# Expert stage: weight rows without a split are split like the rest, every sixth low part goes to GpSimd, and results are added in groups of three pairs

## The chip, the cores and the metric

The kernel runs on one core of one Trainium2 chip, as one program in one launch. The metric is the device time of that program in microseconds (us). Kernels are compared by the median of several runs.

## The reference

The model has two blocks. The change is in the last part of the first: sixteen experts, each of which takes the 64 tokens of 512 that the router rates highest for it.

```
logits = jnp.einsum('bnd,de->ben', xn, router_w).astype(jnp.float32)
aff = jax.nn.softmax(logits, axis=1)
gate, idx = lax.top_k(aff, cap)                                   # cap = 64
xg = jax.vmap(lambda xs, ix: xs[ix])(xn, idx)                     # 16 experts x 64 x 1024
hid = jax.nn.silu(jnp.einsum('becd,edf->becf', xg, w_gate)) * jnp.einsum('becd,edf->becf', xg, w_up)
y = jnp.einsum('becf,efd->becd', hid, w_down) * gate[..., None].astype(xn.dtype)
scatter = lambda ix, ys: jnp.zeros((n, d), ys.dtype).at[ix.reshape(-1)].add(ys.reshape(-1, d))
return jax.vmap(scatter)(idx, y)
```

All matrices are 1024 x 1024 in float32, three for each expert (`w_gate`, `w_up`, `w_down`). The result, scaled, is added to the residual `h` (512 x 1024). Behind it stand a norm and the second block, two layers of attention and feed-forward, which the change does not touch.

## The kernel before

A float32 product is made from rounded halves: a value x is split into a high part, x rounded to the format `F32R`, and a low part, x minus the high part. TensorE then multiplies the `F32R` parts.

**The experts' weights.** 48 matrices come in rows of 128 x 1024 (512 KB), here called chunks: 8 to a matrix, 24 to an expert, 384 in all. `stream` sets their order, and `moe_load` sends each on the SP queue into one of 19 raw buffers (tiles `mraw`, `raw`, `PT`, `rawx`, `moewk`). `moe_w` takes the next chunk and splits it: ScalarE (ACT) writes the high part (`whi`, `mwhi`), VectorE (DVE) or GpSimd (POOL) subtracts it from the raw chunk to get the low part (`wlo`, `mwlo`). There are four buffer pairs for these parts (three with tag `w`, one with tag `mw`), so that chunk n takes over the pair of chunk n - 4. After a split, the next load is issued into the freed raw buffer.

**Who makes the low part.** A counter n numbers the split chunks. The first five low parts and each with n % `MPOOL` == `MPOOL` - 1 are GpSimd's, the others VectorE's. With `MPOOL` = 9 these are 42 and 294 of 336.

**The direct chunks.** The third chunk of each matrix (k = 2, `DIRECT = (2,)`) isn't split. Its 48 products are made in plain float32 from the raw chunk (64 rows of output), with the unsplit tokens in `XD` or the unsplit hidden values in `hs`; the chunk's raw buffer is free when TensorE has read it.

**The products.** `moe_mm` makes, for each split chunk, four products 128 x 512: the stationary operand holds the high parts of the 64 tokens in its first 64 columns and their low parts in the rest (`XS` for gate and up, `HS` for down). `hidden` adds the two halves while it transposes (product with `J`), applies silu and multiplies; `down` adds the halves with one ACT copy and one VectorE addition for each half of a row (`zt`, `z`).

**Adding to the residual.** Two experts make a pair. `pair_rows` scales the pair's rows, splits them (`yh`, `yl`) and builds a 0/1 matrix (`oht`) that places rows at their tokens. `combine` sums over the pairs in the list `Y` in PSUM, for each of 4 token tiles and 2 halves, and VectorE adds the sum to `h`. `GROUPS = (1, 5, 9, 13)` names the experts behind which this is done: after one pair, then after two pairs, three times; the eighth pair is added in `b2_entry`, the first step of the second block (`add`, then norm, then the first projection).

The program is written in that order, and a scheduling step orders each engine's instructions by its own estimate; waits between engines follow from the data. The stage below is the stretch from 711 to 1275 us of the trace: from the first product of an expert to the last.

Of the kernel before, what the change touches and what calls it, by code (L numbers as in the profile page):

```python
# [8 lines left out]
F32 = mybir.dt.float32  # L9
F32R = mybir.dt.float32r  # L10
# [12 lines left out]
MRAW = 7  # L23
AFTER = (0, 1, 2, 3)
RAWS = MRAW + 12
DIRECT = (2,)
MPOOL = 9
GROUPS = (1, 5, 9, 13)
CAP = 64
EPS = 1e-6  # L30
LN_EPS = 1e-5
# [6 lines left out]
class Net:  # L38
# [904 lines left out]
    def moe_w(self, *key):  # L943

        nc = self.nc
        got, raw = self.raws.pop(0)
        assert got == key
        if key[2] in DIRECT:
            return raw, None
        n = self.cw  # L950
        self.cw += 1
        P, tag, bufs = (self.wp, "w", 3) if n % 4 < 3 else (self.mw, "mw", 1)
        hi = P.tile([128, 1024], F32R, name=tag + "hi", tag=tag + "hi", bufs=bufs)
        lo = P.tile([128, 1024], F32R, name=tag + "lo", tag=tag + "lo", bufs=bufs)
        nc.scalar.copy(hi, raw)  # L955
        eng = nc.gpsimd if n < 5 or n % MPOOL == MPOOL - 1 else nc.vector
        eng.tensor_tensor(lo, raw, hi.bitcast(F32), OP.subtract)  # L957
        self.moe_load()
        return hi, lo
# [27 lines left out]
    def xs_pair(self):  # L987

        nc, mo = self.nc, self.mo2
        XS = [mo.tile([128, 8, 128], F32R, name="XS%d" % i, tag="XS", bufs=3) for i in range(2)]  # L990
        XD = mo.tile([128, max(1, len(DIRECT)), 2, 64], F32, name="XD", tag="XD", bufs=2)
        for q in range(2):
            pt = self.aux()
            for k in range(4):
                o = (4 * q + k) * 128
                nc.tensor.transpose(pt[:, k * 128:(k + 1) * 128], self.xg[:, o:o + 128], self.ident)
            p4 = pt.rearrange("p (k e s) -> p k e s", k=4, e=2)
            ks = slice(4 * q, 4 * q + 4)
            for j, k in enumerate(DIRECT):
                if k // 4 == q:  # L1000
                    nc.scalar.copy(XD[:, j], p4[:, k % 4])
            for i in range(2):
                nc.scalar.copy(XS[i][:, ks, 0:64], p4[:, :, i])
                nc.vector.tensor_tensor(XS[i][:, ks, 64:128], p4[:, :, i], XS[i][:, ks, 0:64].bitcast(F32), OP.subtract)
        return [(XS[i], {k: XD[:, j, i] for j, k in enumerate(DIRECT)}) for i in range(2)]

    def moe_mm(self, wn, e, X, X32):
        nc = self.nc
        pp = [self.mm(), self.mm()]
        for k in range(8):  # L1010
            wh, wl = self.moe_w(wn, e, k)
            for q in range(2):
                c = slice(q * 512, (q + 1) * 512)
                if wl is None:
                    nc.tensor.matmul(pp[q][0:64], X32[k], wh[:, c], start=False, stop=False)
                    continue
                nc.tensor.matmul(pp[q], X[:, k], wh[:, c], start=k == 0, stop=False)  # L1017
                nc.tensor.matmul(pp[q], X[:, k], wl[:, c], start=False, stop=k == 7)  # L1018
            if wl is None:
                self.moe_load()  # L1020
        return pp

    def hidden(self, e, X):

        nc, mo = self.nc, self.mo2
        V = nc.vector
        fT = []
        for m, wn in enumerate(("w_gate", "w_up")):
            pp = self.moe_mm(wn, e, *X)
            g = self.wk[:, 1 + m]  # L1030
            nc.scalar.copy(g[:, 0:512], pp[0])
            nc.scalar.copy(g[:, 512:1024], pp[1])
            pf = self.aux()
            for k in range(8):
                nc.tensor.matmul(pf[:, k * 64:(k + 1) * 64], g[:, k * 128:(k + 1) * 128], self.J, start=True, stop=True)
            fT.append(pf)
        s = mo.tile([128, 512], F32, name="hs", tag="hs", bufs=2)
        nc.scalar.activation(s, fT[0], AF.Silu)
        V.tensor_tensor(s, s, fT[1], OP.mult)
        HS = mo.tile([128, 8, 128], F32R, name="HS", tag="HS", bufs=2)  # L1040
        s3 = s.rearrange("p (k n) -> p k n", k=8)
        nc.scalar.copy(HS[:, :, 0:64], s3)
        V.tensor_tensor(HS[:, :, 64:128], s3, HS[:, :, 0:64].bitcast(F32), OP.subtract)
        return HS, {k: s3[:, k] for k in DIRECT}

    def down(self, e, HS):

        nc, mo = self.nc, self.mo2
        pp = self.moe_mm("w_down", e, *HS)
        if e % 2 == 0:  # L1050
            self.z = mo.tile([128, 1024], F32, name="z", tag="z", bufs=1)
        r = slice(64 * (e % 2), 64 * (e % 2) + 64)
        for q in range(2):
            t = mo.tile([64, 512], F32, name="zt", tag="zt", bufs=1)
            nc.scalar.copy(t, pp[q][64:128])
            nc.vector.tensor_tensor(self.z[r, q * 512:(q + 1) * 512], pp[q][0:64], t, OP.add)

    def pair_rows(self, p):

        nc, mo = self.nc, self.mo2  # L1060
        V = nc.vector
        z = self.z
        yh = mo.tile([128, 1024], F32R, name="yh", tag="yh", bufs=2)
        yl = mo.tile([128, 1024], F32R, name="yl", tag="yl", bufs=2)
        V.scalar_tensor_tensor(z, z, self.gd[:, p:p + 1], self.g2, op0=OP.mult, op1=OP.mult)
        nc.scalar.copy(yh, z)
        V.tensor_tensor(yl, z, yh.bitcast(F32), OP.subtract)
        pb = self.aux()
        for s in range(2):
            sel = self.s16[0:16, 2 * p + s:2 * p + s + 1].to_broadcast([16, 64])  # L1070
            nc.tensor.matmul(pb[64 * s:64 * s + 64], sel, self.posT[0:16].bitcast(F32), start=True, stop=True)
        oht = mo.tile([128, 512], F32R, name="oht", tag="oht", bufs=2)
        V.tensor_scalar(oht, pb, self.rowi, None, op0=OP.is_equal)
        return yh, yl, oht

# [10 lines left out]
    def experts(self):  # L1086
# [17 lines left out]
        def finish(e):  # L1104
# [3 lines left out]
            Y.append(self.pair_rows(e // 2))  # L1108
            if e not in GROUPS:
                return  # L1110
# [734 lines left out]
    def ffn(self, l):  # L1845
# [18 lines left out]
        def ready(k):  # L1864
            kept[k] = hidden(k)
# [6 lines left out]
        for q in range(2):  # L1872
# [4 lines left out]
            def mms(t, i, w, kks=(0, 1)):  # L1877
                ts = slice(t * 128, (t + 1) * 128)
                for kk in kks:
                    k, o = 2 * i + kk, slice(kk * 512, (kk + 1) * 512)  # L1880
                    h = w[2 + kk]
                    self.mm3(ps[t], h[0][:, ts], h[1][:, ts], w[0][:, o], w[1][:, o], k == 0, k == 21)

            rows = lambda i: (hidden(2 * i), hidden(2 * i + 1))
            for i in range(last):
                h = rows(i)
# [189 lines left out]
```

## Time and profile before

| | |
|---|---|
| runs | 3185.0 us median of three (3178.12 to 3187.54) |
| profiled execution | 3183.61 us, of which span 3181.8 us |
| TensorE (PE) busy over the span | 3039.0 us (96%) |
| VectorE (DVE) | 2247.8 us (71%) |
| ScalarE (ACT) | 1587.9 us (50%) |
| GpSimd (POOL) | 379.9 us (12%) |
| granted TensorE clock, mean | 0.981 of full |

Busy time of an engine is the time in which at least one of its instructions ran. These shares are means over stages that differ: what the change is worth is read from the expert stage alone, some 18% of the span. A wait for several things is put down to the one that came last.

### The profile page before, as it was taken

How to read it: one execution, taken by the hardware profiler on the slowest of the kernel's cores; microseconds unless marked ns; L12 is line 12 of the kernel's file. 1: busy time of each engine (PE TensorE's matmuls, PEld its weight loads, DVE VectorE, ACT ScalarE, POOL GpSimd, SP SyncE). 2: the span in 40 equal slices, each digit the busy share in tenths (PEclk: the TensorE clock that was granted, in tenths of full speed). 3: DMA queues.
4: the chain of work that ended last, by engine and by line, in shares of the span. 5: the costliest groups of instructions: out<-in, count | busy, mean ns of one | idle time of the engine just before them, and what ended most of it. 6: DMA issues, size and time to landing. Idle time of an engine off the chain costs nothing. (4 is left out here: it accounts for less than half of the span.)

```text
span 3181.8 us, 43471 instructions
## 1 busy us (share of the span) xinstructions
PE 3039.0 (96%) x16242; PEld 2477.6 (78%) x16242; DVE 2247.8 (71%) x3782; ACT 1587.9 (50%) x2711; POOL 379.9 (12%) x295
## 2 busy tenths in 40 slices
PE   7999999969999999699999999999999999999998
PEld 4888777756655666678787789998878777789986
DVE  7778665468988888777565488873676655688854
ACT  6445432228766776365353435551465444445541
POOL 1454200032112121200011000000000011000000
PEclk9999999979999999899999999999999999999999
DMA  5112245549999997311215333332312224333332
GB/s 196 54 47 71 83 143 192 198 179 396 374 345 342 350 370 271 101 62 58 87 56 166 97 117 99 109 105 93 106 54 74 76 93 148 100 106 107 107 100 79
DMA packets 140781, 470.05 MB, mean 148 GB/s; under 512 B 16269, under 2 KB 20365, under 8 KB 140569
## 3 DMA queue, kind: packets, MB, share of 16 engines
q1 hardware_dynamic: 139416, 463.08, 41.7%
q0 software_dynamic: 1152, 4.19, 0.4%
q8 instruction: 127, 2.08, 0.3%
q14 instruction: 86, 0.70, 0.1%
HBM read 456.71 MB, written 10.50 MB: 147 GB/s over the span
## 5 line engine op out<-in xcount | busy, mean ns | idle before, releaser
L107 DVE TENSOR_TENSOR wlo<-raw,whi 128x1024 fp32r<-128x1024 f32 (+4 forms) x340 | 379.9, 1120 | 306.4 <-ACT whi L106 305.0
L106 ACT CAST whi<-raw 128x1024 fp32r<-128x1024 f32 (+4 forms) x340 | 317.6, 936 | 416.7 <-PE mm L116 165.0
L115 PE MATMUL mm<-xTh,whi 128*128 128x512 f32 (+2 forms) x880 | 344.7, 392 | 5.6 <-ACT P L1245 2.6
L116 PE MATMUL mm<-xTh,wlo 128*128 128x512 f32 (+3 forms) x880 | 341.3, 388 | 0.0
L117 PE MATMUL mm<-xTl,whi 128*128 128x512 f32 (+2 forms) x880 | 339.1, 386 | 0.4 <-DVE xTl L267 0.2
L115 PE MATMUL mm<-whi,xTh 128*128 128x512 f32 (+1 forms) x536 | 208.1, 390 | 2.5 <-DVE zt L562 2.1
L116 PE MATMUL mm<-whi,xTl 128*128 128x512 f32 (+1 forms) x536 | 208.2, 389 | 0.5 <-DVE xTl L1150 0.5
L117 PE MATMUL mm<-wlo,xTh 128*128 128x512 f32 (+1 forms) x536 | 204.7, 387 | 0.0
L115 PEld LDWEIGHTS mm<-xTh,whi 128*128 128x128 f32 (+1 forms) x880 | 165.8, 188 | 46.5 <-ACT P L1245 4.2
L117 PEld LDWEIGHTS mm<-xTl,whi 128*128 128x128 f32 (+1 forms) x880 | 165.4, 188 | 36.9 <-DVE xTl L267 1.5
L116 PEld LDWEIGHTS mm<-xTh,wlo 128*128 128x128 f32 (+1 forms) x880 | 165.9, 189 | 34.3 <-issue 1.4
L1018 PE MATMUL mm<-wlo,XS 128*128 128x512 f32 x336 | 114.3, 413 | 18.0 <-DVE wlo L957 11.7
L1409 POOL TENSOR_TENSOR ql<-q,qh 128x512 fp32r<-128x512 f32 x16 | 20.7, 1291 | 853.0 <-ACT qh L1408 853.0
L115 PEld LDWEIGHTS mm<-whi,xTh 128*128 128x128 f32 x536 | 102.1, 191 | 23.4 <-DVE zt L562 2.5
L116 PEld LDWEIGHTS mm<-whi,xTl 128*128 128x128 f32 x536 | 102.1, 191 | 20.3 <-DVE xTl L1150 1.0
L117 PEld LDWEIGHTS mm<-wlo,xTh 128*128 128x128 f32 x536 | 102.0, 190 | 19.7
L957 DVE TENSOR_TENSOR wlo<-mraw,whi 128x1024 fp32r<-128x1024 f32 x82 | 108.6, 1341 | 8.9 <-ACT whi L955 7.7
L1017 PE MATMUL mm<-whi,XS 128*128 128x512 f32 x336 | 111.2, 406 | 0.9 <-ACT whi L955 0.9
L955 ACT CAST whi<-mraw 128x1024 fp32r<-128x1024 f32 x96 | 97.7, 1049 | 15.2 <-PE mm L1017 12.5
L1245 ACT ACTIVATE P<-mm,smv 128x512 f32<-128x512 f32 x128 | 88.1, 690 | 31.2 <-DVE P L1533 16.1
L107 DVE TENSOR_TENSOR flo<-fs,fhi 128x1024 fp32r<-128x1024 f32 x80 | 97.6, 1220 | 5.7 <-ACT fhi L106 4.6
L116 PE MATMUL mm<-whi,hl 128*128 128x512 f32 x248 | 96.6, 390 | 0.0
(827 smaller groups left out, 8620.3 us busy)
## 6 DMA issues: line engine op xcount, KB each, us to landing
raw<-w_f SPq DMA_DIRECT2D x92, 512.0 KB
raw<-w_gate SPq DMA_DIRECT2D x68, 512.0 KB
mraw<-w_gate SPq DMA_DIRECT2D x52, 512.0 KB
mraw<-w_down SPq DMA_DIRECT2D x49, 512.0 KB
araw<-ada SPq DMA_DIRECT2D x48, 512.0 KB
mraw<-w_up SPq DMA_DIRECT2D x43, 512.0 KB
rawu<-w_f SPq DMA_DIRECT2D x40, 512.0 KB
PT<-w_up SPq DMA_DIRECT2D x30, 512.0 KB
```

Source lines behind the costliest of these rows:

```text
L106: nc.scalar.copy(hi[:, :n], raw[:, :n])
L107: nc.vector.tensor_tensor(lo[:, :n], raw[:, :n], hi[:, :n].bitcast(F32), OP.subtract)
L115: mm(out, ah, bh, start=first, stop=False)
L116: mm(out, al, bh, start=False, stop=False)
L117: mm(out, ah, bl, start=False, stop=last)
L955: nc.scalar.copy(hi, raw)
L957: eng.tensor_tensor(lo, raw, hi.bitcast(F32), OP.subtract)
L1017: nc.tensor.matmul(pp[q], X[:, k], wh[:, c], start=k == 0, stop=False)
L1018: nc.tensor.matmul(pp[q], X[:, k], wl[:, c], start=False, stop=k == 7)
L1245: nc.scalar.activation(P, s, AF.Exp, bias=v[:, 8 + i:9 + i], accum_out=v[:, 16 + i:17 + i])
L1409: nc.gpsimd.tensor_tensor(ql, q, qh.bitcast(F32), OP.subtract)
```

## The change

Direct chunks are gone: all 384 are split, and the code and tiles for the unsplit path (`XD`, `X32`) leave. `MPOOL` goes from 9 to 6: GpSimd makes 69 low parts (the first five and n = 5, 11, 17, ...) and VectorE 315. `GROUPS` becomes (5, 11): three pairs are summed in PSUM at once, twice, and the last two pairs are added in `b2_entry`. The tiles `yh`, `yl` and `oht` have three buffers in place of two.

```diff
-DIRECT = (2,)
-MPOOL = 9
-GROUPS = (1, 5, 9, 13)
+MPOOL = 6
+GROUPS = (5, 11)
...
         got, raw = self.raws.pop(0)
         assert got == key
-        if key[2] in DIRECT:
-            return raw, None
         n = self.cw
...
         XS = [mo.tile([128, 8, 128], F32R, name="XS%d" % i, tag="XS", bufs=3) for i in range(2)]
-        XD = mo.tile([128, max(1, len(DIRECT)), 2, 64], F32, name="XD", tag="XD", bufs=2)
...
-            for j, k in enumerate(DIRECT):
-                if k // 4 == q:
-                    nc.scalar.copy(XD[:, j], p4[:, k % 4])
...
-    def moe_mm(self, wn, e, X, X32):
+    def moe_mm(self, wn, e, X):
...
             for q in range(2):
                 c = slice(q * 512, (q + 1) * 512)
-                if wl is None:
-                    nc.tensor.matmul(pp[q][0:64], X32[k], wh[:, c], start=False, stop=False)
-                    continue
                 nc.tensor.matmul(pp[q], X[:, k], wh[:, c], start=k == 0, stop=False)
                 nc.tensor.matmul(pp[q], X[:, k], wl[:, c], start=False, stop=k == 7)
-            if wl is None:
-                self.moe_load()
...
-        yh = mo.tile([128, 1024], F32R, name="yh", tag="yh", bufs=2)
-        yl = mo.tile([128, 1024], F32R, name="yl", tag="yl", bufs=2)
+        yh = mo.tile([128, 1024], F32R, name="yh", tag="yh", bufs=3)
+        yl = mo.tile([128, 1024], F32R, name="yl", tag="yl", bufs=3)
...
-        oht = mo.tile([128, 512], F32R, name="oht", tag="oht", bufs=2)
+        oht = mo.tile([128, 512], F32R, name="oht", tag="oht", bufs=3)
```

Outside the expert stage and its exit, each engine's order is the same. Three places show what moves. The first is TensorE at the start of the first expert, around the third chunk of its `w_gate`; before (line 1015 is the direct product, 1017 and 1018 are those with the high and the low part):

```order
L1017 MATMUL mm<-whi,XS_5884 128x512
L1018 MATMUL mm<-wlo,XS_5884 128x512
L1017 MATMUL mm<-whi,XS_5884 128x512
L1018 MATMUL mm<-wlo,XS_5884 128x512
L1015 MATMUL mm<-mraw,XD 64x512 x2
L1017 MATMUL mm<-whi,XS_5884 128x512
L1018 MATMUL mm<-wlo,XS_5884 128x512
L1017 MATMUL mm<-whi,XS_5884 128x512
L1018 MATMUL mm<-wlo,XS_5884 128x512
```

The same place in the changed kernel, where 1007 and 1008 are the lines of the two products:

```order
L1007 MATMUL mm<-whi,XS_5884 128x512
L1008 MATMUL mm<-wlo,XS_5884 128x512
L1007 MATMUL mm<-whi,XS_5884 128x512
L1008 MATMUL mm<-wlo,XS_5884 128x512
L1007 MATMUL mm<-whi,XS_5884 128x512
L1008 MATMUL mm<-wlo,XS_5884 128x512
L1007 MATMUL mm<-whi,XS_5884 128x512
L1008 MATMUL mm<-wlo,XS_5884 128x512
```

The two float32 products of the direct chunk have left, and four products of a split chunk stand there.

The second place is GpSimd from its first low parts to the third gather of tokens (the DMA row), before:

```order
L957 TENSOR_TENSOR wlo<-mraw,whi 128x1024 x3
L957 TENSOR_TENSOR mwlo<-mraw,mwhi 128x1024
L980 DMA moewk<-xf_scratch,idx 128x1024 x2
L957 TENSOR_TENSOR wlo<-mraw,whi 128x1024
L957 TENSOR_TENSOR wlo<-raw,whi 128x1024
L957 TENSOR_TENSOR wlo<-mraw,whi 128x1024
L980 DMA moewk<-xf_scratch,idx 128x1024
```

And in the changed kernel:

```order
L954 TENSOR_TENSOR wlo<-mraw,whi 128x1024 x3
L954 TENSOR_TENSOR mwlo<-mraw,mwhi 128x1024
L977 DMA moewk<-xf_scratch,idx 128x1024 x2
L954 TENSOR_TENSOR wlo<-mraw,whi 128x1024 x2
L954 TENSOR_TENSOR mwlo<-PT,mwhi 128x1024
L954 TENSOR_TENSOR wlo<-rawx,whi 128x1024
L954 TENSOR_TENSOR mwlo<-mraw,mwhi 128x1024
L977 DMA moewk<-xf_scratch,idx 128x1024
```

Five low parts stand ahead of the third gather where three stood.

The third place is TensorE at the exit of the stage, from the last expert's last products to the transposes of the residual (`ident`,`h`), before (1082 and 1083 are `combine`'s products):

```order
L1017 MATMUL mm<-mwhi,HS 128x512 x2
L1018 MATMUL mm<-mwlo,HS 128x512 x2
L1082 MATMUL aux<-yh,oht 128x512 x4
L1083 MATMUL aux<-yl,oht 128x512 x4
L1082 MATMUL aux<-yh,oht 128x512
L1083 MATMUL aux<-yl,oht 128x512
...
L1146 MATMUL aux<-ident,h_5183 128x128 x8
L115 MATMUL mm<-whi,xTh 128x336
L115 MATMUL mm<-mch_10530,xTh 128x336
```

And in the changed kernel:

```order
L1007 MATMUL mm<-mwhi,HS 128x512 x2
L1008 MATMUL mm<-mwlo,HS 128x512 x2
L1070 MATMUL aux<-yh,oht 128x512 x4
L1071 MATMUL aux<-yl,oht 128x512 x4
L1070 MATMUL aux<-yh,oht 128x512
L1071 MATMUL aux<-yl,oht 128x512
...
L1134 MATMUL aux<-ident,h_5183 128x128 x8
L114 MATMUL mm<-whi,xTh 128x336
L114 MATMUL mm<-mch_10754,xTh 128x336
L1134 MATMUL aux<-ident,h_5184 128x128 x8
```

Behind the last expert product there were 16 products of `combine`, and now there are 24 (8 of the 16 that were added stand further up, among the last expert's products); and the second tile's transposes stand ahead of the first tile's projection.

## Rows read from the trace of the kernel before

**Rows 1.** Busy time by engine in the stage (711 to 1275 us), with its sum.

```profile
core 0: us, PE busy (x) PEld busy (x) DVE busy (x) ACT busy (x) POOL busy (x), PEclk, DMA share, GB/s
...
744.00:1200.00 456.00, 429.01 (x1831) 284.38 (x1830) 391.36 (x392) 332.28 (x410) 91.11 (x35) 1.00 0.96 363
...
sum 564.00, PE 532.11 PEld 354.25 DVE 485.25 ACT 411.03 POOL 114.62; mean PE 177.37 PEld 118.08 DVE 161.75 ACT 137.01 POOL 38.21
```

**Rows 2.** The same stretch, the experts' low parts alone (line 957).

```profile
sum 564.00, DVE 382.25 POOL 107.86; mean DVE 127.42 POOL 35.95
```

**Rows 3.** Lines 957 and 955: duration of one in ns, min/median/max, first and last start.

```profile
L957 DVE TENSOR_TENSOR wlo<-mraw,whi x82: 1203/1216/3427, 714.4 to 1270.6; 128x1024 fp32r<-128x1024 f32 x82
L957 POOL TENSOR_TENSOR wlo<-mraw,whi x14: 2332/2394/5708, 687.5 to 1266.1; 128x1024 fp32r<-128x1024 f32 x14
L955 ACT CAST whi<-mraw x96: 1036/1048/1065, 686.4 to 1268.2; 128x1024 fp32r<-128x1024 f32 x96
```

**Rows 4.** Timeline of TensorE: start, length, instruction, count, [idle before <-releaser].

```profile
833.38 1.93 PE L1015 MATMUL mm<-rawx,XD 128*64 128x512 f32 x4
835.24 0.73 PE L1017 MATMUL mm<-mwhi,XS 128*128 128x512 f32 x2
...
836.28 0.63 PE L1017 MATMUL mm<-whi,XS 128*128 128x512 f32 x2
836.75 0.63 PE L1018 MATMUL mm<-wlo,XS 128*128 128x512 f32 x2
```

**Rows 5.** Timeline at GpSimd's low parts: first and last of 38, three between.

```profile
713.49 2.36 POOL L957 TENSOR_TENSOR wlo<-mraw,whi 128x1024 fp32r<-128x1024 f32 x1 [1.15 <-ACT whi L955]
...
800.42 3.08 POOL L957 TENSOR_TENSOR wlo<-rawx,whi 128x1024 fp32r<-128x1024 f32 x1 [11.82 <-ACT whi L955]
801.26 0.69 DVE L1056 TENSOR_TENSOR z<-mm,zt 64x512 f32<-64x512 f32 x1
801.98 2.60 DVE L957 TENSOR_TENSOR mwlo<-rawx,mwhi 128x1024 fp32r<-128x1024 f32 x1
...
1020.93 5.71 POOL L957 TENSOR_TENSOR wlo<-mraw,whi 128x1024 fp32r<-128x1024 f32 x1 [11.42 <-ACT whi L955]
1020.96 1.22 DVE L1067 TENSOR_TENSOR yl<-z,yh 128x1024 fp32r<-128x1024 f32 x1
1022.09 2.35 DVE L957 TENSOR_TENSOR wlo<-raw,whi 128x1024 fp32r<-128x1024 f32 x2
...
1101.24 2.47 DVE L1115 TENSOR_TENSOR h<-h,aux 128x512 f32<-128x512 f32 x4
1101.38 2.41 POOL L957 TENSOR_TENSOR wlo<-mraw,whi 128x1024 fp32r<-128x1024 f32 x1 [14.30 <-PE aux L1083]
...
1266.07 2.37 POOL L957 TENSOR_TENSOR wlo<-mraw,whi 128x1024 fp32r<-128x1024 f32 x1 [11.38 <-PE mm L1017]
```

**Rows 6.** Timeline of TensorE behind the part of 1020.93.

```profile
1026.69 1.22 PE L1018 MATMUL mm<-wlo,XS 128*128 128x512 f32 x2 [3.95 <-POOL wlo L957]
```

**Rows 7.** VectorE's additions to the residual in the stage: count, busy, mean ns.

```profile
L1115 DVE TENSOR_TENSOR h<-h,aux 128x512 f32<-128x512 f32 x32 | 20.4, 676 | 0.1
```

**Rows 8.** Busy time of two other stretches, columns as in rows 1.

```profile
480.00:560.00 80.00, 80.00 (x348) 63.47 (x347) 43.84 (x42) 20.02 (x26) 0.95 (x1) 1.00 0.61 196
740.00:800.00 60.00, 59.77 (x260) 40.64 (x259) 54.44 (x52) 47.99 (x58) 14.29 (x5) 1.00 1.02 409
```

**Rows 9.** What the SP queue (the loads) waited for in the stage: total us, times, longest.

```profile
SPq L941 <- DVE wlo L957: 191.9, 167, 5.7
...
SPq L941 <- PE mm L1015: 57.3, 37, 5.3
```

**Rows 10.** Timeline of TensorE at the exit of the stage.

```profile
1279.79 2.08 PE L1082 MATMUL aux<-yh,oht 128*128 128x512 f32 x4 [5.75 <-ACT yh L1066]
...
1304.43 1.97 PE L1146 MATMUL aux<-ident,h 128*128 128x128 f32 x8 [18.06 <-DVE h L1224]
```

More of the change, by code (lines that the diff above doesn't have):

```diff
@@ L1004, in xs_pair @@
                 nc.vector.tensor_tensor(XS[i][:, ks, 64:128], p4[:, :, i], XS[i][:, ks, 0:64].bitcast(F32), OP.subtract)
-        return [(XS[i], {k: XD[:, j, i] for j, k in enumerate(DIRECT)}) for i in range(2)]
-    def moe_mm(self, wn, e, X, X32):
+        return XS
+    def moe_mm(self, wn, e, X):
         nc = self.nc
@@ L1028, in hidden @@
         for m, wn in enumerate(("w_gate", "w_up")):
-            pp = self.moe_mm(wn, e, *X)
+            pp = self.moe_mm(wn, e, X)
             g = self.wk[:, 1 + m]
@@ L1043, in hidden @@
         V.tensor_tensor(HS[:, :, 64:128], s3, HS[:, :, 0:64].bitcast(F32), OP.subtract)
-        return HS, {k: s3[:, k] for k in DIRECT}
+        return HS
     def down(self, e, HS):
         nc, mo = self.nc, self.mo2
-        pp = self.moe_mm("w_down", e, *HS)
+        pp = self.moe_mm("w_down", e, HS)
         if e % 2 == 0:
```

## The prediction

> **What bounds the stage now.** I first read the busy time by engine for the stretch of the experts, 711 to 1275 us, 564 us in all [rows 1]. TensorE is busy for 532.1 us, 94%; VectorE for 485.25, 86%; ScalarE for 411.0, 73%. The page's means over the whole program say nothing of the change, since no other stage uses the lines that it touches. TensorE looks like the bound. But look at GpSimd beside VectorE. The view of line 957 by source gives what one low part takes: 1.216 us in the median on VectorE, at least 2.332 and in the median 2.394 on GpSimd, and on both engines up to several us [rows 3]. The timeline shows why some are long [rows 5]. The GpSimd part that starts at 800.42 ends at 803.50. VectorE's addition out of PSUM at 801.26 takes its 0.69 us beside it, but the low part that VectorE starts at 801.98 takes 2.60 and ends at 804.58, 1.08 behind GpSimd's end. At 1020.93 it goes the other way: GpSimd's part takes 5.71 us because VectorE runs three SBUF subtractions first (1020.96 to 1024.44), and it ends 2.20 behind them. At 1101.38 four additions out of PSUM (2.47 us for four) run beside a GpSimd part that takes 2.41, and neither slows. So in this trace a subtraction of two SBUF tiles on one of the two engines stands still while the other has one; additions that read PSUM don't. For low parts, the two engines are one resource.
>
> How full is it? I laid the timeline rows of both engines over one another: 38 GpSimd parts between 713.49 and 1266.07 [rows 5] and VectorE's 485.25 us. One or the other is busy for 513.0 of 564 us, 91%. So two resources are each over 90% full, and four pairs of buffers stand between them; each loses some to the other.
>
> **The change, part by part.**
>
> Direct chunks on TensorE. A direct chunk holds TensorE from 833.38 to 835.24, 1.86 us; two products of a split chunk go by in 0.467 (836.28 to 836.75), four in 0.934 [rows 4]. 48 chunks give back 48 x 0.926 = 44.4 us. Eight `combine` products move out of the stage, 8 x 0.23 = 1.9. TensorE's bill falls from 532.1 to 485.8.
>
> ScalarE. 48 more high parts at 1.048 us [rows 3] are 50.3 us: 411.0 becomes 461. The copies into `XD` go; I give nothing for them. Both lie in the 27% of the stage in which ScalarE stands idle. If that cover were gone, the price would be the 50 us, but at 461 us ScalarE stays below both other resources.
>
> Low parts. VectorE makes 315 in place of 294: 21 x 1.216 = 25.5 us more. In the stage GpSimd makes 65 in place of 38 (four of the 42 and of the 69 are made before it). What one more GpSimd part costs the joint resource I take from rows 1, 2 and 5. VectorE's 294 parts should take 294 x 1.216 = 357.5 us; they took 382.25 [rows 2], so 24.8 us, 0.65 for each GpSimd part, is VectorE held up. And 513.0 - 485.25 = 27.7 us, 0.73 a part, is GpSimd at work while VectorE has nothing to do. Together 1.38 us a part, 27 x 1.38 = 37.3. The bounds: 0.65, if VectorE's empty time would have stood anyway, and 2.33, if nothing that VectorE does fits beside a part [rows 3]. I take 1.38, since that is what the 38 parts show, and the mix beside them stays alike.
>
> Additions to the residual. Two groups in place of four within the stage: 32 additions become 16, each 0.676 us [rows 7], 10.8 us less on VectorE. The `combine` products are as many as before. More buffers for `yh`, `yl` and `oht` cost no time.
>
> Joint bill after: 513.0 + 25.5 + 37.3 - 10.8 = 565.0 us; bounds 545.3 (at 0.65) and 590.7 (at 2.33).
>
> A rule of the Trainium skill bears on the price of a part: its page "SBUF — State Buffer", section "Who interferes with whom", says that a VectorE instruction with two SBUF inputs and a GpSimd instruction that reads SBUF exclude one another, and that the one issued first holds the ports for the whole of its instruction. The exclusion agrees with rows 5; the order does not at 1020.93, where GpSimd was first by 0.03 us and waited for three VectorE instructions. By the rule alone each part costs its whole length, and the bill is the 590.7; by the rows it is 565.0.
>
> How full can the joint resource be? Where one engine leads clearly it fills its time: TensorE is busy for 80.00 of 80 us from 480 to 560, with VectorE at 55% [rows 8]. Now it is 91% full beside a TensorE at 94%. Afterwards TensorE has 485.8 us of work, a good 80% of the stage, so it holds the others up less often, but buffers are still few. Between 91% and 100% I take the middle, 95.5%: 565.0 / 0.955 = 591.6 us, 27.6 more than 564. TensorE's gain is thus not collected: low parts come late, and TensorE waits for them.
>
> Queues. On SP, 57.3 us of waiting for direct products to free a raw buffer go over into waits for low parts, of which there are 191.9 us already [rows 9]; ScalarE's and VectorE's waits name no load, so nothing there reaches the path. On GpSimd the gathers of tokens queue behind more parts, five and not three before the third. They are issued two pairs ahead, and a late one costs at most one part, 2.4 to 5.7 us [rows 3].
>
> Exit. Eight more products behind the last expert are 1.9 us, twice that at the half clock. VectorE now weaves the norms of four tiles into one another, and the first projection waits for the norms already: 18.06 us before 1304.43 [rows 10]. I give 4 us, between nothing and 9 (half of that wait).
>
> Sum, against the profiled execution's 3183.6 us (1.8 outside its span): 3183.6 + 27.6 + 4 = 3215.2. The median of the runs is 1.4 above that execution, so I forecast 3216 us.
>
> **Rivals.**
>
> Faster. TensorE's 94% is the true bound, and the new parts find place in VectorE's 79 idle us: a part costs 0.65 and the joint bill is 545.3. At 99% full that is 551 us, 13 less, and with no loss at the exit 3171. It decides from the point where 545.3 fits into 564 us, a fill of 96.7%. For it speaks the idle time, and that taking 44 us off TensorE also lets buffers come free sooner. Against it: the other 1.7 us of each new part, 45 us in all, would have to lie beside VectorE work that does not stand still, and of that there are now 16 additions fewer. 13 in 100.
>
> No change. The loads set the pace. 384 chunks of 512 KB are 201 MB; at the 363 GB/s of the stage's middle, with the DMA engines at 0.96 [rows 1], they take 555 us, before and after. Against it: 409 GB/s from 740 to 800 [rows 8], and the SP queue's waits for buffers [rows 9], which say that the loads wait for the splits. The case takes in a bill and a fill that happen to cancel (565 at nearly 100%). About 3185; 17 in 100. The skill's same page, section "A bandwidth-pool intuition that's wrong", gives about 358 GB/s from HBM for a core; by that the loads would take 562 us, which is the whole stage. The 60 us at 409 GB/s speak against it as a limit here.
>
> Much slower. A GpSimd part is served late when VectorE is full, as at 1020.93, and TensorE then stands for 3.95 us [rows 6]; its buffer pair is kept, ScalarE can't refill it, and the fill stays at 91%: 565.0 / 0.91 = 621 us, 57 more, 3245 with the exit. The bill of 590.7 at 95.5% gives 619, the same. 20 in 100.
>
> **How the numbers follow.** My forecast (slower by 10 to 50 us) has 50 in 100. The range takes in the faster case to 3168 and the much slower one to 3258. About 0.3%, 10 us, is what a measurement of this kernel can tell from no change: faster by more 0.13, within it 0.17, slower 0.70.
>
> **What the profile after would show.** In the stretch of the stage, TensorE's share falls to some 82% and its idle time stands before line 1008, ended by VectorE or GpSimd low parts; VectorE's share rises to 90% or more; medians of one low part stay at 1.22 and 2.4, but more of them are long; the stage lasts some 590 us. A split chunk in the place of a direct one takes 0.93 on TensorE. My step on the joint resource is wrong if TensorE stays above 92% with a shorter stage; the step on fill, if the joint busy share is at 91% or at 99%; the step on the part's price, if held-up time for each GpSimd part is far from 0.65 us. Behind the exit, all else should take as long as before.

## The result and the profile after

The changed kernel takes 3255.45 us in the median of 4 runs (3252.01 to 3259.77), the kernel before 3181.56 beside it (4 runs, 3176.76 to 3187.54). The ratio is 1.0235, with a 95% interval of 1.0223 to 1.0248: 74 us slower. The forecast had been 31 us slower, with 3258 as the upper end of its range.

The whole loss lies in the experts' stage. From the first to the last expert product the timeline has 563.3 us before and 637.6 after (707.4 to 1344.9), 74.3 more; from there to the program's end it has 1907.8 and 1908.3. (The stage begins 3.3 us earlier in the later trace, so the two profiled executions differ by 71.5.) Busy time by engine in 708 to 1346 us (columns as in [rows 1]):

```profile
708.00:741.00 33.00, 29.36 (x140) 22.22 (x139) 28.07 (x34) 27.26 (x35) 14.70 (x7) 0.99 0.93 339
741.00:1271.00 530.00, 440.62 (x1891) 321.27 (x1890) 450.08 (x409) 377.51 (x454) 175.23 (x59) 0.94 0.89 320
1271.00:1346.00 75.00, 61.74 (x237) 41.78 (x235) 64.08 (x51) 51.28 (x61) 22.12 (x8) 0.91 0.59 204
sum 638.00, PE 531.73 PEld 385.27 DVE 542.23 ACT 456.05 POOL 212.05; mean PE 177.24 PEld 128.42 DVE 180.74 ACT 152.01 POOL 70.68
```

No engine is full over the stage: TensorE 83%, VectorE 85%, ScalarE 71%. The granted clock of the middle, 1.00 before, is 0.94, and the loads go at 320 GB/s in place of 363. Before, TensorE had been at 94% [rows 1]. What it waits for stands in the view of line 1008, the product of the low part:

```profile
its engine sat idle before it (us, times) until:
  DVE wlo L954: 109.5, 133
  POOL wlo L954: 69.1, 43
  POOL mwlo L954: 48.7, 25
  DVE mwlo L954: 28.1, 38
```

These idle times count the weight loads too, so they add up to more than TensorE's 106 idle us; their order is what matters: low parts of both engines, none of anything else above 1 us. The low parts themselves (line 954, as line 957 in [rows 2, 3]): busy time in the same stretch, then durations in ns.

```profile
sum 638.00, DVE 441.00 POOL 205.30; mean DVE 147.00 POOL 68.43
```

```profile
L954 DVE TENSOR_TENSOR wlo<-mraw,whi x92: 1203/1215/3433, 712.0 to 1339.9; 128x1024 fp32r<-128x1024 f32 x92
...
L954 POOL TENSOR_TENSOR wlo<-mraw,whi x16: 2337/2458/9101, 684.0 to 1313.1; 128x1024 fp32r<-128x1024 f32 x16
L954 POOL TENSOR_TENSOR mwlo<-mraw,mwhi x13: 2338/2883/7747, 690.9 to 1339.2; 128x1024 fp32r<-128x1024 f32 x13
```

The shortest and the usual ones have hardly moved; the longest of GpSimd have, from 5.71 us [rows 3] to 9.10. VectorE's 315 low parts in the stage would take 383 us at 1.216 and take 441. Laying both engines' timeline rows over one another again, one or the other is busy for 584.7 of 637.6 us, 91.7%.

One late part shows how the loss spreads. The timeline of the changed kernel from 849 to 862 us:

```profile
849.20 2.34 DVE L954 TENSOR_TENSOR wlo<-rawx,whi 128x1024 fp32r<-128x1024 f32 x2
...
850.53 7.75 POOL L954 TENSOR_TENSOR mwlo<-mraw,mwhi 128x1024 fp32r<-128x1024 f32 x1 [4.08 <-PE mm L1007]
...
851.47 1.21 DVE L954 TENSOR_TENSOR wlo<-moewk,whi 128x1024 fp32r<-128x1024 f32 x1
...
852.60 3.48 DVE L954 TENSOR_TENSOR wlo<-mraw,whi 128x1024 fp32r<-128x1024 f32 x3
...
853.76 0.63 PE L1007 MATMUL mm<-whi,XS 128*128 128x512 f32 x2
...
858.34 0.72 PE L1008 MATMUL mm<-mwlo,XS 128*128 128x512 f32 x2 [3.94 <-POOL mwlo L954]
...
858.87 0.58 ACT L1019 COPY moewk<-mm 128x512 f32<-128x512 f32 x1 [5.01 <-PE mm L1008]
...
859.68 1.06 PE L1007 MATMUL mm<-whi,XS 128*128 128x512 f32 x2
859.83 1.06 ACT L952 CAST mwhi<-mraw 128x1024 fp32r<-128x1024 f32 x1
...
860.92 1.23 DVE L954 TENSOR_TENSOR mwlo<-mraw,mwhi 128x1024 fp32r<-128x1024 f32 x1 [4.84 <-ACT mwhi L952]
```

GpSimd starts at 850.53 and ends at 858.28. VectorE serves itself first, low part behind low part until 856.08; GpSimd ends 2.20 behind that, about the 2.34 us that one of its parts takes alone. It is the last chunk of a matrix, so ScalarE's copy of the product (line 1019) waits for it, 5.01 us. The next high part (859.83) stands behind that copy in ScalarE's queue, and VectorE has nothing to subtract until 860.92, 4.84 us. So TensorE (3.94 us), ScalarE and VectorE stand still for one part. The clock pays as well: two products take 1.06 us at 859.68 in place of the 0.63 at 853.76. Two stretches, the wait and what follows it (the third column from the end is the granted clock):

```profile
853.00:858.00 5.00, 1.39 (x6) 0.78 (x5) 3.08 (x3) 0.86 (x1) 5.00 (x1) 1.00 0.87 329
859.00:861.50 2.50, 2.50 (x8) 1.95 (x7) 0.58 (x1) 2.50 (x4) 0.00 (x0) 0.50 0.88 310
```

Behind the wait TensorE runs at the lower of its two levels, 1.2 GHz, for the whole of the second stretch, 2.5 us.

### The profile page after: what moved, and what is told of

Read it like the earlier page. It is cut to its first block, busy times and chain, and to the rows that moved or that the text cites. A ratio compares the mean times of both kernels' runs of the same rounds, so it can differ in the third digit from the quotient of the medians.

```text
span 3253.2 us, 43681 instructions
## 1 busy us (share of the span) xinstructions
PE 3033.0 (93%) x16242; PEld 2504.3 (77%) x16242; DVE 2301.8 (71%) x3787; ACT 1632.5 (50%) x2751; POOL 476.6 (15%) x322
## 5 line engine op out<-in xcount | busy, mean ns | idle before, releaser
L1008 PE MATMUL mm<-wlo,XS 128*128 128x512 f32 x384 | 146.4, 458 | 58.3 <-DVE wlo L954 29.3
L954 DVE TENSOR_TENSOR wlo<-mraw,whi 128x1024 fp32r<-128x1024 f32 x92 | 132.7, 1458 | 38.1 <-ACT whi L952 37.2
L1008 PEld LDWEIGHTS mm<-wlo,XS 128*128 128x128 f32 x384 | 71.0, 208 | 104.6 <-DVE wlo L954 58.2
L1397 POOL TENSOR_TENSOR ql<-q,qh 128x512 fp32r<-128x512 f32 x16 | 20.6, 1290 | 855.5 <-ACT qh L1396 855.5
L1007 PE MATMUL mm<-whi,XS 128*128 128x512 f32 x384 | 132.8, 422 | 2.0 <-ACT whi L952 1.9
L952 ACT CAST whi<-mraw 128x1024 fp32r<-128x1024 f32 x108 | 110.8, 1050 | 17.3 <-issue 6.7
```

## The experiments

Two causes were in question: the 27 further GpSimd low parts, or something that the rest of the change brings (groups of three pairs, no direct chunks). When the first had been found, the question became how a GpSimd part costs so much. Each ratio is to the kernel before, run beside it on the same chip (medians 3179.75 to 3180.51 us); shares of a stage go from its first to its last expert product.

**Fewer GpSimd parts in the changed kernel.** Every ninth low part in place of each sixth:

```
-MPOOL = 6
+MPOOL = 9
```

> All chunks split as in the changed kernel, but GpSimd makes each ninth low part: 43 in the stage, not 65, and VectorE 337, not 315. Theory A (VectorE and GpSimd are one resource for low parts, and a part costs it 2.1 us on GpSimd and 1.2 on VectorE, at a fill of 91.7%): 22 x (2.13 - 1.22) = 20 us off the joint bill, 22 us off the time, some 3233 us. Theory B (VectorE's own load is what sets the pace, so GpSimd's parts relieve it): 22 x 1.22 us more for VectorE, some 3280 us. Theory C (the missing direct chunks alone cost the time, whoever makes the low parts): 3255 us, no change.

Measured: 3215.97 us, 1.0111 (1.0094 to 1.0128). And none but the first five:

```
-MPOOL = 6
+MPOOL = 1000
```

> All chunks split, and all low parts but the first five on VectorE. Theory A: 64 parts go over, 64 x 0.91 = 58 us off the joint bill, 64 us off the time, some 3192 us. Theory B: 78 us more for VectorE, some 3340 us. Theory C: 3255 us.

Measured: 3157.77 us, 0.9925 (0.9908 to 0.9942), faster than before. So 69, 47 and 5 GpSimd parts give 3255, 3216 and 3158: 1.8 us for each of the first 22 taken away, 1.4 for each of the other 42. Both gains, 39 and 98 us, are well above the 22 and 64 that the first theory gave. Without GpSimd's parts the whole loss, and more, is gone. The stage of the second kernel and its low parts:

```profile
707.00:1250.00 543.00, 502.79 (x2264) 360.02 (x2262) 523.74 (x555) 453.80 (x547) 8.99 (x8) 1.00 0.96 363
...
sum 543.00, DVE 441.71 POOL 2.40; mean DVE 441.71 POOL 2.40
```

VectorE makes 379 parts here in 441.7 us, where 315 took 441.0 in the changed kernel: **GpSimd's 64 parts took nothing off VectorE's time.** VectorE is now the bound, busy for 96.5%.

**The same in the kernel before.** First each sixth low part there too (61 GpSimd parts in place of 42), then none but the first five:

```
-MPOOL = 9
+MPOOL = 6
```

> The kernel before with its direct chunks, but each sixth low part on GpSimd: 57 in the stage, not 38. Theory A: 19 x 0.91 = 17 us on the joint bill, some 19 us more than before, 3201 us. Theory B: 19 x 1.22 = 23 us less for VectorE, some 3160 us. Theory C: as before, 3182 us.

Measured: 3213.08 us, 1.0103 (1.0086 to 1.0120).

```
-MPOOL = 9
+MPOOL = 1000
```

> The kernel before with its direct chunks, and all low parts but the first five on VectorE. The three kernels measured so far say that a GpSimd part costs 1.5 to 1.8 us of time more than a VectorE part. If that holds here, 37 parts are worth some 60 us: 3121 us. If TensorE then sets the pace (its busy time of 532 us fills the stage), the stage can't fall below some 530 us: 3148 us. If direct chunks are worth nothing once GpSimd is out, it comes to the time of the same kernel without them, 3158 us.

Measured: 3165.58 us, 0.9948 (0.9931 to 0.9965). 19 parts more cost 33 us, 1.7 each; 37 fewer bring 15, 0.4 each, since TensorE with its direct chunks then takes over as the bound:

```profile
708.00:1256.00 548.00, 530.84 (x2278) 357.18 (x2277) 483.82 (x525) 411.03 (x509) 8.94 (x8) 0.99 0.94 359
```

TensorE is busy for 97% of the stage. With GpSimd out in both, the rest of the change is no loss: 3165.58 and 3157.77, with intervals that overlap.

The kernels with GpSimd at work show what the parts of the change are worth beside it. Each sixth part in place of each ninth costs 33 us with the direct chunks (3180 to 3213) and 39 without them (3216 to 3255). Taking the direct chunks out, and nothing else, costs 39 us at each sixth part (3213.08 to 3251.86, a kernel given below) and nothing where GpSimd is out (3165.58 and 3163.34, below too, with intervals that overlap). So the setting of `MPOOL` is only about half of the loss. The other half is the 48 further chunks to split, eight of them on GpSimd. They cost time beside GpSimd's parts and none without them.

**Groups of three pairs alone, in the kernel before.**

```
-GROUPS = (1, 5, 9, 13)
+GROUPS = (5, 11)
...
-        yh = mo.tile([128, 1024], F32R, name="yh", tag="yh", bufs=2)
+        yh = mo.tile([128, 1024], F32R, name="yh", tag="yh", bufs=3)
```

(`yl` and `oht` alike.)

> The kernel before with the sums in PSUM over three pairs (twice, the last two pairs in the second block's entry) and three buffers for the pair's rows. Theory A: 16 additions, 10.8 us, leave the joint bill: some 10 us less, 3172 us, if TensorE at 94% lets it through. Theory C and a bound on TensorE: within 5 us of before.

Measured: 3193.13 us, 1.0039 (1.0027 to 1.0052). The 11 us expected from 16 fewer additions did not come; the stage is 8 us longer and what follows it 5. The two kernels below with the old groups don't settle it: with GpSimd out the old groups are 5.6 us slower than the new ones, with GpSimd's 69 parts 3.6 us faster, and in both cases the intervals overlap. The size of this edit depends on what else the stage waits for, and it is small beside the loss.

**The old groups with GpSimd out** (the changed kernel with `MPOOL = 1000`), as the base of the next two:

```
-GROUPS = (5, 11)
+GROUPS = (1, 5, 9, 13)
...
-        yh = mo.tile([128, 1024], F32R, name="yh", tag="yh", bufs=3)
+        yh = mo.tile([128, 1024], F32R, name="yh", tag="yh", bufs=2)
```

> The changed kernel with all low parts but five on VectorE, and the sums in PSUM as before: GROUPS (1, 5, 9, 13), two buffers for the rows. If sums over three pairs cost what they cost in the kernel before (13 us), 3145 us. If VectorE is the bound now, its 16 additions more are 11 us: 3169 us.

Measured: 3163.34 us, 0.9943 (0.9926 to 0.9959).

**GpSimd subtractions that nobody needs.** To the kernel just named, 64 unused subtractions are added; VectorE makes every low part as before, and nothing waits for `junk`:

```
+        if n % 6 == 5:
+            self.idle(cp)
...
+        junk = self.mo2.tile([128, 1024], F32, name="junk", tag="junk", bufs=1)
+        g = self.nc.gpsimd.tensor_tensor(junk, self.g2, self.g2, OP.subtract)
+        self.behind(g, cp, "one at each sixth chunk")
```

> As e6, and GpSimd does 64 subtractions of a 128 x 1024 tile from itself, one behind the high part of each sixth chunk, into a tile that nobody reads: added work whose result is left unused. Nothing waits for it, so what it costs is exclusion alone. If GpSimd's parts cost time because VectorE stands still meanwhile: 64 x 1.5 us or more, some 100 us above e6, 3245 us. If they cost time because a part comes late to TensorE and keeps its buffers: within 20 us of e6.

Measured: 3259.26 us, 1.0250 (1.0227 to 1.0272): 95.9 us for 64 subtractions, 1.50 each. Busy time in the stage, of all and of the low parts alone, in the base and then in this kernel (`mod` in the third fence is the tile that holds `g2`):

```profile
708.00:1256.00 548.00, 505.37 (x2274) 361.84 (x2274) 534.33 (x573) 456.99 (x549) 9.01 (x8) 1.00 0.95 361
...
sum 548.00, DVE 442.16 POOL 2.41; mean DVE 442.16 POOL 2.41
```

```profile
708.00:1352.00 644.00, 540.94 (x2275) 384.86 (x2275) 624.08 (x573) 463.55 (x549) 214.84 (x72) 0.95 0.87 307
...
sum 644.00, DVE 523.54 POOL 2.41; mean DVE 523.54 POOL 2.41
```

The unused subtractions by tile, durations in ns:

```profile
L963 POOL TENSOR_TENSOR junk<-mod x64: 1895/2688/7849, 713.6 to 1345.8; 128x1024 f32<-128x1024 f32 x64
```

The same 573 instructions of VectorE take 624 us in place of 534, 81 of the 90 us more in its low parts. VectorE stays 97% busy; it is not late, it stands still inside its instructions. In its timeline:

```profile
898.85 2.18 POOL L963 TENSOR_TENSOR junk<-mod 128x1024 f32<-128x1024 f32 x1 [7.39 <-ACT mwhi L952]
899.20 2.92 DVE L954 TENSOR_TENSOR wlo<-mraw,whi 128x1024 fp32r<-128x1024 f32 x1
```

The low part ends 1.09 us behind GpSimd's end, close to the 1.204 of the shortest low part, as if it had begun only then.

**The same places, but GpSimd only writes.** In place of each unused subtraction two memsets of `junk`, behind the same high part:

```
-        g = self.nc.gpsimd.tensor_tensor(junk, self.g2, self.g2, OP.subtract)
+        g = self.nc.gpsimd.memset(junk, 0.0)
+        self.nc.gpsimd.memset(junk, 0.0)
```

> In place of each of the 64 unused GpSimd subtractions (which had brought 3163 us to 3259), two GpSimd memsets of the same tile, 0.95 us each, behind the same high part. They read nothing. Exclusion by reads of SBUF: VectorE's low parts are not held up, the time stays at 3160 to 3170 us. If the mere presence of a GpSimd instruction that writes SBUF, or the wait it brings, costs the time: 3240 us or more.

Measured: 3163.71 us, 0.9948 (0.9931 to 0.9964): nothing, beside a base of 3163.34. Busy time of the low parts in the stage:

```profile
sum 548.00, DVE 441.93 POOL 2.40; mean DVE 441.93 POOL 2.40
```

In the base it was 442.16. The memsets by tile, in ns:

```profile
L963 POOL MEMSET junk<- x64: 949/956/966, 713.2 to 1250.7; 128x1024 f32 x64
L964 POOL MEMSET junk<- x64: 952/956/967, 714.2 to 1251.7; 128x1024 f32 x64
```

GpSimd is at work for 1.91 us at each sixth chunk, as long as the shortest of the subtractions, and neither engine lengthens the other's instructions. So the 1.50 us are not the price of GpSimd's presence, its issue or its writes. They belong to what a subtraction has and a memset hasn't, most likely its reads of SBUF; no run reads SBUF on GpSimd without subtracting.

**A fifth pair of buffers.** If lateness is what four pairs can't cover, a fifth should help. The changed kernel with old groups and two buffers of `yh`, `yl` and `oht`, which frees the room, and then with the pair:

> The changed kernel with MPOOL 6 and the sums in PSUM as before: e8 without its fifth pair of buffers. By e6 against e2 (5.6 us more with the old groups): 3261 us, and the fifth pair is worth nothing. If the pair is worth 20 us: 3280 us. If sums over three pairs cost 13 us as in e4: 3242 us, and the pair makes it worse.

Measured, without the pair: 3251.86 us, 1.0223 (1.0206 to 1.0240).

```
-        P, tag, bufs = (self.wp, "w", 3) if n % 4 < 3 else (self.mw, "mw", 1)
+        P, tag, bufs = (self.wp, "w", 3) if n % 5 < 3 else (self.mw, "mw", 2)
```

> The changed kernel with MPOOL 6, sums in PSUM as before (GROUPS (1, 5, 9, 13)), and a fifth pair of buffers for high and low parts. Without the fifth pair I expect 3242 us of it (3255 less the 13 of the groups). If a late GpSimd part costs time because it keeps one of four pairs: 40 us less or more, 3200 us or below. If the engines' exclusion costs the time: 10 us less at most, 3232 us or above.

Measured, with it: 3259.59 us, 1.0242 (1.0223 to 1.0261), not faster than without (7.7 us slower in the medians, with intervals that overlap). A fifth pair doesn't help.

**The place of a part within its matrix.** The kernel with GpSimd out, but one part of each matrix on GpSimd, first at its fourth chunk of eight, then at its last (52 and 53 parts in all, all but the first five in the same pair of buffers):

```
-        eng = nc.gpsimd if n < 5 or n % MPOOL == MPOOL - 1 else nc.vector
+        eng = nc.gpsimd if n < 5 or n % 8 == 3 else nc.vector
```

> All chunks split; GpSimd makes the first five low parts and that of the fourth chunk (k = 3) of each matrix, 52 in all. By 1.53 us a part (98 us for 64 between e2 and the changed kernel) 47 more parts than e2 come to 3158 + 72 = 3230 us. If only exclusion counts, e9 and e10 agree within 5 us. If it counts that a late part delays TensorE's end of a matrix, and with it ScalarE's copy of the product, behind which the next high parts queue, a part in the middle of a matrix is cheap: 3205 us or less.

Measured: 3207.95 us, 1.0084 (1.0067 to 1.0100).

> As e9, but the part of the last chunk (k = 7) of each matrix, 53 in all; both take the same buffers. By exclusion alone the same as e9 within 5 us, some 3230 us. By lateness at a matrix's end: 25 us or more above e9, 3235 to 3260 us.

Measured (`n % 8 == 7`): 3241.35 us, 1.0184 (1.0167 to 1.0201). The same work four chunks later costs 33 us more. The waits of ScalarE's copy of the product in the first and in the second kernel (total us, times, longest):

```profile
ACT moewk L1019 <- PE mm L1008: 43.0, 18, 3.8
```

```profile
ACT moewk L1019 <- PE mm L1008: 58.5, 23, 5.0
...
DVE wlo L954 <- ACT whi L952: 49.6, 48, 4.9
```

That is the sequence seen at 850.53: in the second kernel the longest waits of the copy and of VectorE, 5.0 and 4.9, are as long as the 5.01 and 4.84 there. Last, about as many parts as the changed kernel has, 68 to its 69, but none at a matrix's last chunk:

```
+        eng = nc.gpsimd if n < 5 or n % 8 == 3 or n % 24 == 13 else nc.vector
```

> The changed kernel's buffers, groups and number of GpSimd low parts (69), but at chunk 3 of each matrix and chunk 5 of each third one, never at chunks 0, 6 and 7, where each sixth chunk falls in three of eight cases or so. If lateness at a matrix's end carries a third or more of the loss: 3208 + 17 x 1.5 = 3233 us, between 3225 and 3240. If the number of parts alone sets the price: 3255 us, as in the changed kernel, 3248 or more.

(Two things are misstated there: the number is 68, and the places of each sixth chunk are chunks 5, 3, 1 and 7 of a matrix in turn, counted from 0, so a quarter of the changed kernel's parts, 16, are last chunks.) Measured: 3218.34 us, 1.0118 (1.0101 to 1.0135): 37 us less than the changed kernel with one part fewer, and better than the 3225 to 3240 expected.

```profile
709.00:1314.00 605.00, 524.52 (x2266) 373.44 (x2266) 546.42 (x495) 453.58 (x549) 189.98 (x71) 0.96 0.90 326
...
sum 605.00, DVE 438.68 POOL 182.75; mean DVE 438.68 POOL 182.75
```

VectorE's low parts take as long as in the changed kernel; GpSimd's own are shorter by 22.5 us, 182.75 against 205.30, and the waits between shrink.

**A better kernel.** Where VectorE is the bound, a few direct chunks should pay: the kernel with GpSimd out, and one direct chunk in `w_down` alone, 16 in all.

```
+        if key[0] == "w_down" and key[2] == 2:
+            return raw, None
```

> e2 with one direct chunk left in each w_down (16, not 48), a search for a better kernel: VectorE is busy for 524 of 543 us in e2's stage, TensorE for 503. 16 x 1.22 = 19 us leave VectorE and 16 x 0.93 = 15 us come to TensorE: 505 and 518. If the fuller of the two sets the time: some 6 us less, 3152 us. If the two hold one another up: 3158 us or more.

Measured: 3153.31 us, 0.9915 (0.9898 to 0.9932), the fastest median here: 26 us below the kernel before beside it, 102 below the changed one. It is 4.5 us below the kernel with GpSimd out alone, but their intervals overlap. Its stage lasts 538 us, with TensorE 94.7 and VectorE 94.5% busy:

```profile
708.00:1244.00 536.00, 507.38 (x2259) 355.55 (x2259) 506.23 (x535) 436.93 (x529) 8.70 (x8) 1.00 0.96 366
```

## Why the prediction was right in sign and wrong in size

The forecast counted 27.6 us for the stage; it was 74.3. The mechanism, that VectorE and GpSimd are one resource for low parts and TensorE's gain is not collected, was right. Two terms of its sum were wrong: the price of a GpSimd part was too low, and the fill too high. What came true is the rival "much slower": parts served late when VectorE is full, and a fill that stays near 91%. Two of the signs that the prediction had named against itself appeared: the fill, and held-up time well above 0.65 us a part. VectorE's share, expected at 90% or more, came out at 85%, since the stage grew.

**TensorE.** Its forecast share, 82%, came out at 83%. But the bill was not 485.8: with GpSimd out it is 502.8 at a clock of 1.00, and taking the direct chunks out alone brought 25 us (530.84 to 505.37), not 44. A product that had to wait is shown longer (two took 0.72 us at 858.34, against 0.63 in [rows 4]), and there are now more waits, so busy time is no bill once an engine has stopped being full. How much of the missing 17 us this makes up, no run shows. It did not decide the outcome.

**ScalarE.** 461 us forecast, 456 found, and idle for 29% of the stage. What the step missed is its queue: the copy of a product stands ahead of the next high parts, and through it one late low part reaches VectorE.

**The price of a GpSimd part: the term that was mis-sized first.** By the prediction's own reading VectorE is held up for 441.0 - 315 x 1.216 = 58 us by 65 parts, 0.89 each where 0.65 was taken, and GpSimd works alone for 42.9 us, 0.66 each where 0.73 was. The joint bill is 584.7, not 565.0, near the upper bound of 590.7: from 513.0 + 25.5 - 10.8 = 527.7 it rose by 57, 2.1 us for each further part in place of 1.38.

But that reading was itself too low. It took the lengths of 294 low parts from their busy time. In a row of low parts each starts before the last has ended, here 1.14 us apart at a length of 1.22, and busy time counts what overlaps once:

```profile
744.53 1.22 DVE L957 TENSOR_TENSOR mwlo<-raw,mwhi 128x1024 fp32r<-128x1024 f32 x1
745.67 1.22 DVE L957 TENSOR_TENSOR wlo<-raw,whi 128x1024 fp32r<-128x1024 f32 x1
```

The kernel before with GpSimd out shows what low parts take without it, 1.18 us each:

```profile
708.00:1256.00 548.00, 390.65 (x331) 2.36 (x1) 0.99 0.94 359
```

By this measure GpSimd's 38 parts in the kernel before had held VectorE's low parts up by 382.25 - 294 x 1.18 = 35 us, 0.93 each. And from that kernel to the kernel before, the joint bill, found by the same laying over one another, rises from 485.4 to 513.0 us for 37 parts. That is 0.75 each, on top of the 1.18 that each would have taken on VectorE: 1.9 us a part. So a part cost 1.9 us already there, and 27 at that price bring the forecast's bill from 565.0 to 579.0. In the changed kernel the same reckoning, with 525.8 for the joint bill with GpSimd out and 441.7 us for 379 low parts, gives 2.1: 1.14 in VectorE's low parts, 0.3 in its other instructions (101 us beside 82 with GpSimd out) and 0.66 alone. The 1.14 is also why GpSimd's help brings VectorE nothing: a part that is given away saves 1.17 us and costs about as much.

The exclusion behind this is now shown and not only read: 1.50 us of time for each subtraction on GpSimd, 1.40 of it inside VectorE's instructions (624.08 against 534.33 us), and nothing for a memset. The Trainium skill's page "SBUF — State Buffer", section "Who interferes with whom", makes just this difference, between a GpSimd instruction that reads SBUF and one that only writes it, and the runs agree (3259.26 against 3163.71 us). Its other half, that the first to be issued holds the ports for its whole instruction, does not fit the part at 850.53, behind whose start VectorE began and ended four low parts (851.47, and three from 852.60) before GpSimd had finished. In both that case and the one at 1020.93 a VectorE instruction was still running when GpSimd's started, and the next ones went ahead of it.

**The fill: the second.** At 95.5% the joint bill of 584.7 would have given 612 us; the stage took 637.6, a fill of 91.7%. The view that a fuller resource loses less had been taken from a stretch in which one engine led [rows 8]. It holds for one engine alone: VectorE without GpSimd is 96.5% busy, and 97.5% with the old groups. It does not hold for two engines that take turns and wait for one another's order: the kernel with 68 parts off the ends of the matrices is at 94.5% (570.6 of 604.0 us), the kernel with the parts at the ends at 92.5% with fewer of them. The place of the parts is worth 33 us (52 against 53 parts) and 37 us (68 against 69). Buffers, which the prediction named for the low fill, are not the reason as far as one more pair tells: with it the fill is 92.9%, without it 94.1%.

The two steps account for it: 584.7 in place of 565.0 is 20.6 us at the forecast's fill, and the lower fill another 25.4, together 46 of the 46.7 missed in the stage.

**Additions, queues, loads, exit.** The 16 additions take 0.68 us each, as priced; what they free can't be told from the runs. The loads follow: their rate falls to 320 GB/s where low parts are late, and in the fastest kernel it is 366 GB/s over a stage of 538 us. So they don't set the pace of the changed kernel, and the rival "no change" is out. In the changed kernel no wait of the stage names a gather of tokens. The 358 GB/s of the Trainium skill's page "SBUF — State Buffer", section "A bandwidth-pool intuition that's wrong", would make the loads 562 us. That page of the Trainium skill works the figure out as a stack's rate divided between two cores. Here one core runs, and the measurement, 366 over a stage and 409 over 60 us [rows 8], decides against it as a limit. The exit had 4 us and took 0.5 more. The wait for the norms, ahead of the first projection, grew from 18.06 to 21.09 [rows 10], but the stretch as a whole did not:

```profile
1350.18 2.07 PE L1070 MATMUL aux<-yh,oht 128*128 128x512 f32 x4 [5.25 <-ACT yh L1054]
...
1378.71 1.97 PE L1134 MATMUL aux<-ident,h 128*128 128x128 f32 x8 [21.09 <-DVE h L1212]
```

**What stays open.** Of the 97.7 us between the changed kernel and the one with GpSimd out, 94 lie in the stage. The joint bill accounts for 61 of them ((584.7 - 525.8) / 0.968, the fill with GpSimd out), the lower fill for the other 33. What makes the fill is shown only in part: the place of the parts is worth 33 to 37 us, but it acts on the bill as well, and no run holds the rest apart, the falls of the clock among it (0.94 in the mean of the stage). Why groups of three cost 13 us in the kernel before is open too.

## What to carry to other kernels

Before work is shared between VectorE and GpSimd, add up what VectorE takes for its own instructions with and without GpSimd's: here 441 us for 315 parts with GpSimd's help and 441.7 for all 379 alone, so the help was worth nothing, and taking it away was the edit that brought most. Don't set busy time, which counts an overlap once, against lengths of single instructions: the price of a part came out at 1.38 us that way, and at 1.9 against a kernel without such parts. Nor take the fill of a single full engine for two that alternate. A late instruction costs most where other queues stand behind its result: put slow parts where nobody's in-order queue waits for them, in the middle of a matrix and not at its end.

## What the runs showed of the hardware that was not expected

VectorE's run of low parts, each started before the last had ended, keeps a GpSimd subtraction waiting for several of its instructions, though GpSimd's started ahead of these: parts of up to 9.10 us in the changed kernel, of 2.34 when undisturbed. GpSimd memsets of 128x1024 float32 (0.95 us each, 128 of them) beside the same VectorE work lengthen nothing. And a wait of TensorE of 3.94 us is followed here by at least 2.5 us at the lower clock level, so that such a wait costs more than its length: with GpSimd out the stage's granted clock is 1.00, with its 65 parts 0.94.
